# Storing the lower parts of split projection weights to device memory in the first half of the sequence and loading them in the second

## The chip, the cores and the metric

The kernel runs on one core of one Trainium2 chip. The metric is the device time of one execution in microseconds (us); smaller is better. Engines are named as in the profile: PE (TensorE matmul), PEld (its weight loads), DVE (VectorE), ACT (ScalarE), POOL (GpSimd), SP (SyncE, which issues all DMAs of this kernel).

## What is computed

A two-layer trunk on one sequence of 1024 tokens with 1024 channels, all in float32. Layer 0 is an RWKV-7 time mixer, layer 1 a diagonal state-space layer with a GLU; each is followed by a dense MLP (1024 to 4096 to 1024), and each of the four sub-layers by a layer norm. The part that matters here is the time mixer's projections:

```python
xx = jnp.pad(x, ((0, 0), (1, 0), (0, 0)))[:, :-1] - x
xr = x + xx * mu[0]; xw = x + xx * mu[1]; xk = x + xx * mu[2]
xv = x + xx * mu[3]; xa = x + xx * mu[4]; xg = x + xx * mu[5]
r = xr @ wr; k = xk @ wk; v = xv @ wv
w_pre = w0 + jnp.tanh(xw @ w1) @ w2
a = jax.nn.sigmoid(a0 + (xa @ a1) @ a2)
g = jax.nn.sigmoid(xg @ g1) @ g2
...
state = state * w_t + (state a_t) b_t + v_t k_t   # per head and token
...
h = layer_norm(ALPHA * h + (o * g) @ wo)
```

Token t of the recurrence needs r, k, v, w, a of token t and the state of token t-1. The weights are the same for all tokens.

## The kernel before, in words

**Arithmetic.** A float32 product is made of three reduced-precision (float32r) products. Every operand is split (`split`, L145): ACT copies it into a float32r tile, the upper part (`hi`), and DVE subtracts that from the original, which gives the lower part (`lo`). `mm3` (L177) then issues hi·hi, hi·lo and lo·hi into one PSUM tile.

**Weights.** `wload` (L158) brings weights in tiles of 128 x 512 (256 KB): a load to `wraw` on SP's queue (L163; 2 buffers), a cast to `whi` on ACT (L146; 3 buffers), a subtraction to `wlo` on DVE (L147; 3 buffers). The buffers of `whi` and `wlo` come free when PE has done the tile's matmuls. `WLG` (L56) is set so that no subtraction goes to POOL.

**Two halves.** The sequence is cut into two halves of 512 tokens, and `rwkv_proj(H)` (L229) makes the projections of half H with the same weights, so every weight tile is loaded and split once in each half. Through `wload` go, in each half, 2 tiles of `wa2` (`rates`, L369), 2 of `g2a` (`gate`, L384), 16 of `wk` and 16 of `wr` (`square`, L400) and 16 of `wv` (L443): 52 tiles. The results are stored to device memory by SP (`store_out`, L364; L458 for v) and loaded again by the recurrence. A few more weights (`wa1`, `g1a`, `g1c`) are scaled by mu first and go through `scaled` (L295), not through `wload`.

**Recurrence.** `core` (L757) works through 8 units: two head groups by four stretches of 256 tokens. For each: `elem` (L474; loads of r, k, sg, a at L485 and element-wise work), `amat`, `invert` (L585; a long row of small DVE operations at L608 and L610), `kbtrans`, `chain` (L645; the steps that hand the state on; loads of v at L654), `gnorm` (L701). Units 0 to 3 need the first half's projections, units 4 to 7 the second half's.

**Order.** The order on each engine's queue is made by a planner: the program is written with ranks (`rank(...)`, L86; the lower rank goes first), and the planner places instructions by a simulated timeline, by rank and by when buffers come free. Each engine, SP's DMA queue too, then works its list strictly in order. The projections of the second half (L772) and most of those of the first (L767) have rank 100000, so they fill what the units leave. After the projections come `wo`, layer norms, the MLPs and the state-space layer; these have `wload` calls of their own, which the change leaves as they are.

Of the kernel before, what the change touches and what calls it, by code (L numbers as in the profile page):

```python
# [8 lines left out]
F32 = mybir.dt.float32  # L9
# [10 lines left out]
KT = 8  # L20
# [35 lines left out]
WLG = (3, (), 0, 1)  # L56
# [14 lines left out]
def trunk(ctx, tc, A):  # L71
    nc = tc.nc
    V, S, G, PE, SP = nc.vector, nc.scalar, nc.gpsimd, nc.tensor, nc.sync

    cp = ctx.enter_context(tc.tile_pool(name="cp", bufs=1))
    dr = ctx.enter_context(tc.tile_pool(name="dr", bufs=1, space=DRAM))
# [68 lines left out]
    def split(src, hi, lo, e=None):  # L145
        S.copy(hi, src)  # L146
        (e or V).tensor_sub(lo, src, hi.bitcast(F32))  # L147
# [7 lines left out]

    nw = [0]

    def wload(src, kt, n):  # L158
        step = 512 // n
        out = []  # L160
        for k0 in range(0, kt, step):
            raw = wp.tile([128, step, n], F32, tag="wraw", name="wraw", bufs=2)
            SP.dma_start(raw, src[:, k0 : k0 + step])  # L163
            hi = wp.tile([128, step, n], F32R, tag="whi", name="whi")
            lo = wp.tile([128, step, n], F32R, tag="wlo", name="wlo")
            nw[0] += 1
            split(raw, hi, lo, G if nw[0] % WLG[0] in WLG[1] and WLG[2] <= nw[0] < WLG[3] else V)
            out += [(hi[:, k], lo[:, k]) for k in range(step)]
        return out

# [3 lines left out]
    def mmb(p, w, x, **kw):  # L174
        bulk.append((PE.matmul(p, w, x, **kw).ins, x.shape[-1]))  # L175

    def mm3(p, whi, wlo, xh, xl, first, last):  # L177
        mmb(p, whi, xh, start=first, stop=False)
        mmb(p, whi, xl, start=False, stop=False)
        mmb(p, wlo, xh, start=False, stop=last)  # L180
# [18 lines left out]
    def dense(p, w, xs):  # L199
        n = len(xs)  # L200
        for k in range(n):
            mm3(p, w[k][0], w[k][1], xs[k][0], xs[k][1], k == 0, k == n - 1)
# [11 lines left out]
    def psd():  # L214
        return pd.tile([128, HT], F32, tag="d", name="d")
# [13 lines left out]
    def rwkv_proj(H):  # L229
# [21 lines left out]
        def spare(tag, n, bufs, pool=kp):  # L251
            t = pool.tile([128, n, HT], F32R, tag=tag, name="oS", bufs=bufs)
            return [t[:, k] for k in range(n)]
# [9 lines left out]
        def mixes(j, dst=None):  # L263
            for k in range(KT):
                m = tp.tile([128, HT], F32, tag="m", name="m")
                S.mul(m, xs[k][:, 1:], mum[:, j, k : k + 1])
                if k % 4 in VM[H]:
                    V.scalar_tensor_tensor(m, xs[k][:, 0:HT], vec(f"mu{j}", k), m, op0=ALU.mult, op1=ALU.add)
                else:
                    m2 = tp.tile([128, HT], F32, tag="ev", name="m2", bufs=3)  # L270
                    G.tensor_scalar(m2, xs[k][:, 0:HT], vec(f"mu{j}", k), None, op0=ALU.mult)
                    G.tensor_add(m, m, m2)
                if dst:
                    split(m, *dst[k])
                    yield dst[k]
                else:
                    yield operand(m)
# [3 lines left out]
        if H == 0:  # L281
            hi, lo = spare("AT", KT, 1), []
# [8 lines left out]
        if H == 0:  # L291
            with rank(MIXR):
                xm = list(mixes(2))
# [30 lines left out]
        def half_sigmoid(t):  # L324
            G.tensor_scalar(t, t, 0.5, 0.5, op0=ALU.mult, op1=ALU.add)
# [38 lines left out]
        def store_out(out, n, e):  # L364
            (ST if out in STO else SP).dma_start(scr[out][n * 128 : (n + 1) * 128, t0 : t0 + HT], e)

        w2, wg = [None], [None, None]

        def rates(n):  # L369

            if n % 4 == 0:
                w2[0] = wload(A["wa2"][:, n // 4], 4, 128)
            pp = [psd(), psd()]
            for wi, xi in ((0, 0), (0, 1), (1, 0)):
                for j in range(2):
                    js = slice(64 * j, 64 * j + 64)
                    mmb(pp[j], w2[0][n % 4][wi][js], hx[xi][js], start=wi == 0 and xi == 0, stop=wi == 1)
            for j, out in ((0, "sg"), (1, "a")):
                e = tp.tile([128, HT], F32, tag="ev", name="ev", bufs=3)
                S.activation(e, pp[j], AF.Tanh, bias=pvh[:, j, n : n + 1], scale=0.5)  # L380
                half_sigmoid(e)
                store_out(out, n, e)

        def gate(n):  # L384
            if n % 4 == 0:
                wg[0] = wload(A["g2a"][:, n // 4], 4, 128)
                rawb = wp.tile([128, 512], F32, tag="wraw", name="w2raw", bufs=2)
                SP.dma_start(rawb, A["g2b"][:, n * 128 : n * 128 + 512])
                wg[1] = wp.tile([128, 512], F32R, tag="whi", name="w2st")
                S.copy(wg[1], rawb)  # L390
                V.tensor_sub(wg[1][64:128], rawb[64:128], wg[1][64:128].bitcast(F32))
            q = n % 4
            p = psd()
            mm3(p, wg[0][q][0], wg[0][q][1], gx[0], gx[1], True, False)
            mmb(p, wg[1][:, q * 128 : (q + 1) * 128], h2, start=False, stop=True)
            e = tp.tile([128, HT], F32, tag="ev", name="ev", bufs=3)
            S.copy(e, p)
            store_out("g", n, e)

        def square(wn, out, xm, n):  # L400
            p = psd()
            dense(p, wload(A[wn][n], KT, 128), xm)
            e = tp.tile([128, HT], F32, tag="ev", name="ev", bufs=3)
            S.copy(e, p)  # L404
            store_out(out, n, e)

        if H == 0:

            km = xm
            with rank(MIX0R):  # L410
                rm = list(mixes(0, spare0()))
            for n in range(4):
                rates(n)
                square("wk", "k", km, n)
            for n in range(4):
                square("wr", "r", rm, n)
            yield
            for n in range(4, KT):
                rates(n)
                square("wk", "k", km, n)  # L420
            for n in range(4, KT):
                square("wr", "r", rm, n)
            if not GV:
                for n in range(KT):
                    gate(n)
        else:
            for n in range(KT):
                rates(n)
            for n in range(KT):
                gate(n)  # L430
            xm = list(mixes(2))
            for n in range(KT):
                square("wk", "k", xm, n)
            xm = list(mixes(0))
            for n in range(KT):
                square("wr", "r", xm, n)
# [3 lines left out]
        for cb in range(4):  # L440
            pp = [psd(), psd()]
            for k0 in range(0, KT, 2):
                w = wload(A["wv"][cb][:, k0 : k0 + 2], 2, 256)  # L443
                for kk in range(2):
                    k = k0 + kk
                    for tt in range(4):
                        sl = slice(tt * 128, (tt + 1) * 128)
                        o = pp[tt // 2][:, (tt % 2) * 256 : (tt % 2) * 256 + 256]
                        mmb(o, xv[k][0][:, sl], w[kk][0], start=k == 0 and tt % 2 == 0, stop=False,
                                  skip_group_check=True)  # L450
                        mmb(o, xv[k][0][:, sl], w[kk][1], start=False, stop=False, skip_group_check=True)
                        mmb(o, xv[k][1][:, sl], w[kk][0], start=False, stop=k == KT - 1,
                                  skip_group_check=True)
            for h in range(2):
                e = tp.tile([128, 2, 256], F32, tag="ev", name="evv", bufs=3)
                S.copy(e, pp[h].rearrange("p (t n) -> p t n", t=2))
                r0 = t0 + h * 256
                SP.dma_start(scr["v"][r0 : r0 + 256, cb * 256 : (cb + 1) * 256].rearrange("(t p) n -> p t n", p=128), e)  # L458
        if H == 0 and GV:
            for n in range(KT):  # L460
                gate(n)
# [295 lines left out]
    def core():  # L757

        pg = rwkv_proj(0)
        next(pg)  # L760
        bulk.clear()
# [8 lines left out]
        for m in range(8):  # L770
            if m == PB:
                with rank(100000):  # L772
                    run(rwkv_proj(1))
# [591 lines left out]
```

## Time and profile before

| | us |
|---|---|
| median of 3 runs (lowest, highest) | 2771.85 (2769.56, 2778.86) |
| the profiled execution's own time | 2764.91 |
| its span from the first to the last instruction | 2763.2 |
| PE busy | 2604.9 (94%) |
| DVE busy | 1884.5 (68%) |
| ACT busy | 1109.5 (40%) |
| POOL busy | 719.6 (26%) |
| DMA moved | 318.63 MB, 115 GB/s on average |

The span is cut by what runs in it: set-up to 39 us, the first half's `wload` projections from 39 to 300 us, the second half's from 300 to 660 us (the units run beside both), the rest of the units with the first MLP to 1070 us, then MLPs and the state-space layer. A table by stage has, for each engine, its busy time with the number of instructions, and the granted TensorE clock as a share of full speed (PEclk). Matmuls are pipelined, so PE counts as busy also where it runs at a low clock. A line with "who <- whom" says that the first engine sat idle until the second one's instruction ended.

### The profile page before, as it was taken

Reading aid. Unit: us, or ns where it says so; the run is one execution under the profiler, and the core shown is the slowest. Engines: PE = TensorE matmul, PEld = TensorE weight load, DVE = VectorE, ACT = ScalarE, POOL = GpSimd, SP = SyncE. Lnnn points to the kernel's source line nnn. Section 1 sums busy time; section 2 is a strip of 40 time slices with the busy share of each in tenths; the row PEclk is TensorE's granted clock in tenths of the full one; section 3 lists DMA queues with packets and bytes.
Section 4 is the critical chain, followed back from the end, with each engine's and each line's share of the span. In section 5 each row is a group of like instructions: output and inputs, shape, how many; then the busy total and the mean of one; then the engine's idle time right before and its main releaser. Section 6 shows DMA issues by size and latency. Waiting matters only on the chain.

```text
span 2763.2 us, 43707 instructions
## 1 busy us (share of the span) xinstructions
PE 2604.9 (94%) x16582; PEld 2096.5 (76%) x16582; DVE 1884.5 (68%) x3242; ACT 1109.5 (40%) x1952; POOL 719.6 (26%) x601
## 2 busy tenths in 40 slices
PE   7889989889899999989999999999999999999997
PEld 5779767678677877767776788778778887788886
DVE  7487788587787777998658554574765546755556
ACT  5445454544443333334432332344323323533333
POOL 5331664450352303233122001121220101210101
PEclk9989969889889999999999999999999999999998
DMA  3543443344222323555332633223343322333333
GB/s 115 184 147 112 139 162 102 109 138 135 77 81 81 100 85 124 154 145 159 96 122 99 203 96 98 89 88 102 117 160 112 99 96 84 119 96 97 98 95 100
DMA packets 200083, 318.63 MB, mean 115 GB/s; under 512 B 19520, under 2 KB 73920, under 8 KB 199872
## 3 DMA queue, kind: packets, MB, share of 16 engines
q1 hardware_dynamic: 199872, 315.83, 36.6%
q8 instruction: 131, 2.15, 0.3%
q14 instruction: 80, 0.66, 0.1%
HBM read 265.42 MB, written 50.33 MB: 114 GB/s over the span
## 4 chain that ended last, share of the span: by engine, by line
PE 45%; DVE 5%; issue 2%; POOL 1%; DMA 1%; ACT 0%; ACTq 0%; DVEq 0%; POOLq 0%
PE d L175 40%; PE py L1219 1%; PE py L1224 1%; DVE wlo L147 1%; PE pu L152 1%; DVE t L1187 1%; PE pbu L1175 1%; DVE hA L960 0%; DVE hB L960 0%; DVE t L1185 0%; POOL rl L944 0%; PE pq L849 0%; DMA wraw<-in_mw_dram 0%; PE pu L1164 0%; DVE qbuf L147 0%
## 5 line engine op out<-in xcount | busy, mean ns | idle before, releaser
L147 DVE TENSOR_TENSOR wlo<-wraw,whi 128x512 fp32r<-128x512 f32 x720 | 535.6, 745 | 443.7 <-ACT whi L146 424.8
L146 ACT CAST whi<-wraw 128x512 fp32r<-128x512 f32 x720 | 445.7, 620 | 975.4 <-PE d L175 637.2
L175 PE MATMUL d<-qbuf,whi 128*128 128x512 f32 (+1 forms) x2112 | 655.6, 393 | 20.9 <-DVE hA L960 9.4
L175 PEld LDWEIGHTS d<-qbuf,whi 128*128 128x128 f32 x2112 | 390.3, 190 | 117.7 <-DVE hA L960 17.0
L944 POOL TENSOR_TENSOR rl<-rl 128x512 f32<-128x512 f32 x128 | 158.6, 1239 | 1058.4 <-ACT rl L943 1018.1
L175 PE MATMUL d<-qbuf,wlo 128*128 128x512 f32 (+1 forms) x1056 | 409.3, 390 | 8.2 <-DVE wlo L147 8.0
L175 PE MATMUL d<-oAh,whi 128*128 128x512 f32 (+1 forms) x960 | 387.8, 408 | 9.6 <-ACT ev L404 7.2
L175 PE MATMUL d<-oAh,wlo 128*128 128x512 f32 (+1 forms) x960 | 387.2, 406 | 5.3 <-DVE wlo L147 5.1
L175 PE MATMUL d<-oAl,whi 128*128 128x512 f32 (+1 forms) x960 | 385.5, 404 | 1.4 <-DVE oAl L147 1.4
L175 PE MATMUL d<-oBh,wlo 128*128 128x512 f32 x704 | 278.3, 396 | 1.4 <-DVE wlo L147 1.4
L175 PE MATMUL d<-oBh,whi 128*128 128x512 f32 x704 | 278.8, 396 | 0.0
L175 PE MATMUL d<-oBl,whi 128*128 128x512 f32 x704 | 276.1, 392 | 0.0
L175 PEld LDWEIGHTS d<-qbuf,wlo 128*128 128x128 f32 x1056 | 200.6, 190 | 52.8 <-DVE wlo L147 11.7
L175 PEld LDWEIGHTS d<-oAh,whi 128*128 128x128 f32 (+1 forms) x960 | 185.1, 194 | 54.2 <-ACT ev L404 9.2
L175 PEld LDWEIGHTS d<-oAh,wlo 128*128 128x128 f32 (+1 forms) x960 | 184.9, 193 | 49.1 <-DVE wlo L147 8.6
L175 PEld LDWEIGHTS d<-oAl,whi 128*128 128x128 f32 (+1 forms) x960 | 184.8, 193 | 40.6 <-DVE oAl L147 2.1
L960 DVE TENSOR_TENSOR hB<-hB,d 128x512 f32<-128x512 f32 (+1 forms) x256 | 165.2, 650 | 68.9 <-PE d L175 65.8
L960 DVE TENSOR_TENSOR hA<-hA,d 128x512 f32<-128x512 f32 x240 | 162.5, 683 | 54.5 <-PE d L175 52.5
L175 PEld LDWEIGHTS d<-oBh,wlo 128*128 128x128 f32 x704 | 132.5, 188 | 33.8 <-DVE wlo L147 2.0
L175 PEld LDWEIGHTS d<-oBl,whi 128*128 128x128 f32 x704 | 132.7, 188 | 29.4 <-issue 0.5
L175 PEld LDWEIGHTS d<-oBh,whi 128*128 128x128 f32 x704 | 132.7, 189 | 29.1 <-issue 1.5
L147 DVE TENSOR_TENSOR qbuf<-rl,qbuf 128x512 fp32r<-128x512 f32 x128 | 99.0, 774 | 70.3 <-ACT qbuf L146 69.8
(371 smaller groups left out, 3877.1 us busy)
## 6 DMA issues: line engine op xcount, KB each, us to landing
wraw<-in_mw_dram SPq DMA_DIRECT2D x520, 256.0 KB, 2.7
wraw<-in_glu_dram SPq DMA_DIRECT2D x64, 256.0 KB, 2.6
wraw<-in_wk_dram SPq DMA_DIRECT2D x32, 256.0 KB, 3.1
wraw<-in_wr_dram SPq DMA_DIRECT2D x32, 256.0 KB, 3.1
wraw<-in_wv_dram SPq DMA_DIRECT2D x32, 256.0 KB, 3.4
yl<-s_y SPq DMA_DIRECT2D x32, 256.0 KB, 3.1
wraw<-in_wo_dram SPq DMA_DIRECT2D x32, 256.0 KB, 2.8
tb<-tB SPq DMA_DIRECT2D x16, 512.0 KB, 4.9
```

The source lines that it names most:

```text
L146: S.copy(hi, src)
L147: (e or V).tensor_sub(lo, src, hi.bitcast(F32))
L152: PE.matmul(out, x, idt, start=True, stop=True)
L175: bulk.append((PE.matmul(p, w, x, **kw).ins, x.shape[-1]))
L944: G.tensor_mul(r, r, r)
L960: V.tensor_add(z, z, p)
L1175: PE.matmul(p[qs, g2, ri], tb[:, g2, ri, qs], u[:, 2 * g2 + par], start=True, stop=True)
L1187: e.tensor_mul(t2[:, :, ri], x[:, :, 1 - ri], bw[:, l, g0:g1, ri : ri + 1].broadcast_to([128, g1 - g0, n]))
L1219: PE.matmul(p[64 * j : 64 * j + 64, g2], ug[f][:, 2 * g2 + par], tv[:, par, g2], start=g2 == 0, stop=False, skip_group_check=True)
L1224: PE.matmul(p[64 * j : 64 * j + 64, g2], hb[qs, 4 * f + g2, ri, 0:NSC], tcm[qs, g2, ri], start=False, stop=ri == 1, skip_group_check=True)
```

## The change

`wload` takes a key. With a key seen for the first time (first half) the tile is split as before, and its lower part is stored as it is to a tile of its own in device memory (256 KB, on SP's queue). With a key seen before (second half) the lower part is loaded from there into `wlo` on SP's queue, and only the cast to `whi` is made. The five call sites that run once in each half pass a key; the keys are the same in both halves.

```diff
+    low = {}
+
-    def wload(src, kt, n):
+    def wload(src, kt, n, key=None):
         step = 512 // n
         out = []
         for k0 in range(0, kt, step):
+            kept = low.get((key, k0)) if key else None
             raw = wp.tile([128, step, n], F32, tag="wraw", name="wraw", bufs=2)
             SP.dma_start(raw, src[:, k0 : k0 + step])
             hi = wp.tile([128, step, n], F32R, tag="whi", name="whi")
             lo = wp.tile([128, step, n], F32R, tag="wlo", name="wlo")
             nw[0] += 1
-            split(raw, hi, lo, G if nw[0] % WLG[0] in WLG[1] and WLG[2] <= nw[0] < WLG[3] else V)
+            if kept is not None:
+                SP.dma_start(lo.bitcast(F32).rearrange("p k n -> p (k n)"), kept)
+                S.copy(hi, raw)
+            else:
+                split(raw, hi, lo, G if nw[0] % WLG[0] in WLG[1] and WLG[2] <= nw[0] < WLG[3] else V)
+                if key:
+                    low[key, k0] = dr.tile([128, 512], F32, name=f"low{len(low)}")
+                    SP.dma_start(low[key, k0], lo.bitcast(F32).rearrange("p k n -> p (k n)"))
             out += [(hi[:, k], lo[:, k]) for k in range(step)]
         return out
...
-                w2[0] = wload(A["wa2"][:, n // 4], 4, 128)
+                w2[0] = wload(A["wa2"][:, n // 4], 4, 128, f"wa2{n}")
...
-                wg[0] = wload(A["g2a"][:, n // 4], 4, 128)
+                wg[0] = wload(A["g2a"][:, n // 4], 4, 128, f"g2a{n}")
...
-            dense(p, wload(A[wn][n], KT, 128), xm)
+            dense(p, wload(A[wn][n], KT, 128, f"{wn}{n}"), xm)
...
-                w = wload(A["wv"][cb][:, k0 : k0 + 2], 2, 256)
+                w = wload(A["wv"][cb][:, k0 : k0 + 2], 2, 256, f"wv{cb}-{k0}")
```

## Rows read from the trace of the kernel before

**Rows 1.** Busy time by stage: window, PE, PEld, DVE, ACT, POOL, PEclk, DMA share, GB/s

```profile
39.00:300.00 261.00, 237.25 (x1845) 194.90 (x1844) 168.22 (x328) 128.12 (x235) 85.16 (x83) 0.94 0.45 145
300.00:660.00 360.00, 320.44 (x2933) 264.24 (x2932) 280.34 (x512) 171.15 (x320) 178.78 (x149) 0.85 0.40 127
...
1070.00:2763.00 1693.00, 1631.57 (x8504) 1307.97 (x8498) 1077.45 (x1740) 619.76 (x1051) 305.24 (x239) 0.99 0.37 114
```

**Rows 2.** SP's issues in order of time around the second half's first v

```profile
461.04 1.25 SPq L654 DMA_DIRECT2D vsa<-s_v  x2
...
619.18 0.88 SPq L458 DMA_DIRECT2D s_v<-evv  x2
...
622.68 1.33 SPq L654 DMA_DIRECT2D vsa<-s_v  x2
```

**Rows 3.** Groups of DVE's instructions by line, 300 to 660 us

```profile
L147 DVE TENSOR_TENSOR wlo<-wraw,whi 128x512 fp32r<-128x512 f32 x51 | 40.7, 801 | 30.4 <-ACT whi L146 30.2
```

**Rows 4.** What PE waited for, 300 to 660 us (total us, times, longest)

```profile
PE pU L682 <- ACT vsa L679: 5.7, 4, 2.1
...
PE d L175 <- DVE oAl L147: 4.5, 4, 2.5
PE py L747 <- DVE st L685: 4.0, 1, 4.0
PE pss L507 <- DVE AT L570: 3.0, 1, 3.0
PE d L175 <- DVE wlo L147: 2.9, 3, 1.3
```

**Rows 5.** Busy time in three shorter stretches of the second half (columns as in rows 1)

```profile
450.00:490.00 40.00, 38.13 (x294) 30.54 (x292) 35.82 (x90) 17.13 (x33) 13.15 (x10) 1.00 0.57 171
...
500.00:570.00 70.00, 67.76 (x590) 54.50 (x591) 43.51 (x68) 32.77 (x63) 34.21 (x27) 0.89 0.32 102
570.00:600.00 30.00, 19.49 (x135) 16.90 (x134) 24.77 (x40) 13.50 (x24) 18.25 (x13) 0.78 0.43 133
```

**Rows 6.** All instructions on the tile wraw, 39 to 300 us

```profile
L147 DVE TENSOR_TENSOR wlo<-wraw,whi x52: 637/691/1794, 43.5 to 271.2; 128x512 fp32r<-128x512 f32 x52
...
  DMA wraw<-in_wv_dram: 6.7, 2
  DMA wraw<-in_wr_dram: 4.5, 2
...
DMA to landing us min/median/max: 2.5/3.1/4.6
```

**Rows 7.** Issues of SP by tensor, 39 to 260 us: count, size, median us to landing

```profile
s_k<-ev SPq DMA_DIRECT2D x8, 256.0 KB, 2.6
```

**Rows 8.** SP's issues in order of time, one store

```profile
130.11 0.32 SPq L365 DMA_DIRECT2D s_sg<-ev  x1
```

**Rows 9.** What SP's queue waited for, 300 to 660 us

```profile
SPq L163 <- DVE wlo L147: 66.8, 25, 12.8
...
SPq L485 <- DVE KB L538: 19.2, 6, 5.8
```

**Rows 10.** All instructions on the tile wraw, 300 to 660 us

```profile
L163 SPq DMA_DIRECT2D wraw<-in_wv_dram x16: 327/362/954, 565.4 to 652.0; - x16
...
  DMA wraw<-in_wv_dram: 11.2, 4
  DMA wraw<-in_wr_dram: 7.1, 2
...
DMA to landing us min/median/max: 2.5/3.3/6.2
```

**Rows 11.** PE in order of time: full-clock matmuls of one weight tile

```profile
577.43 0.39 PE L175 MATMUL d<-oAh,whi 128*128 128x512 f32 x1
...
577.66 0.40 PE L175 MATMUL d<-oAl,whi 128*128 128x512 f32 x1
```

## The prediction

> **What bounds the kernel now.** First the table by stage [rows 1]. From 1070 us on PE is busy for 1631.6 of 1693 us at a clock of 0.99: nothing is to be had there, and time saved before it simply moves it forward. The first half's projections (39 to 300 us) run PE for 237.3 of 261 us at 0.94. The worst stage is the second half's projections, 300 to 660 us: PE is idle for 360 - 320.4 = 39.6 us, and its clock is 0.85, so of the 320.4 busy us about 0.15 x 320.4 = 48.1 us were lost to the low level (1.2 instead of 2.4 GHz). Some 88 us of this stage are therefore not TensorE work at full speed. DVE is busy there for 280.3 of 360 us, 78%.
>
> Does the stage's end set anything? SP's issues in order of time say so [rows 2]: the recurrence loads v at 461 us and then not before 622.7 us, 3.5 us after the first v of the second half is stored at 619.2 us. The units 4 to 7 wait for these projections, and the first MLP stands behind them on PE. Sooner projections mean sooner everything.
>
> Next, what DVE does in that stage [rows 3]: the subtractions that make `wlo` of the weights are its largest group, 51 with 40.7 us (the 52nd lies past the edge), 40.7 / 280.3 = 14.5% of its work. But PE's waits [rows 4] hardly name them: 2.9 us in 3 times. What they name is the small steps between units and bulk: a lower part of the activations (4.5), the state (4.0), the masked matrix (3.0), and pX's copies (5.7), all of them on DVE or right behind it. DVE works strictly in order, so a weight subtraction hurts through what is queued behind it. The stretches differ too [rows 5]: from 450 to 490 us DVE is busy for 35.8 of 40 us, yet PE for 38.1 at full clock, so there is little to win; from 570 to 600 us DVE has 24.8 of 30 us and PE only 19.5 at 0.78, so there is much.
>
> **The change, part by part.** Every key of the first half is asked for again in the second, so it does what it says: 52 stores, 52 loads, 52 subtractions fewer.
>
> *First half, added: 52 stores of 256 KB.* An issue of such a store occupies SP for 0.32 us [rows 8] and lands after 2.6 us [rows 7]. Each stands on SP's queue behind a wait for its subtraction; the next raw load but one waits for the same subtraction already, as that frees its `wraw`. Behind it stand other loads and the projections' own stores; if each issue delayed something on the path, it would be 52 x 0.32 = 16.6 us, the upper end. The store also holds the `wlo` buffer: 0.32 + 2.6 us after the subtraction, while PE gets to a tile only after those before it in three buffers, so PE releases later than the store and this costs nothing; without that lead it would be 2.9 us per tile. The traffic grows by 52 x 0.262 = 13.6 MB in 261 us, 52 GB/s on 145 [rows 1], 36%. ACT's waits for raw tiles there were 6.7 + 4.5 us [rows 6]; grown by 36% that is 4.0 us. About half of that is covered by buffered tiles, so I take **+2 us**, between 0 (a gain is excluded: nothing is taken off any engine in this half) and 16.6.
>
> *Second half, removed: 52 subtractions on DVE,* 0.80 us each [rows 3]. The bounds: no gain, if all of it lay beside PE's work; 52 x 0.80 = 41.6 us, if all of it were on the path. Between them I go by shares: of PE's 39.6 idle and 48.1 lost us, the part that belongs to 14.5% of DVE's work, 87.7 x 0.145 = 12.7 us. Rows 4 support the lower half of the bounds (most of DVE's work is hidden). I take **-12.7 us**. There is a page on the chip that makes the share larger: the Trainium skill (SBUF — State Buffer, "two separate sides") says that a VectorE instruction with two SBUF inputs and a GpSimd instruction that reads SBUF lock each other out for a whole instruction. The trace agrees in direction: here the subtraction takes 0.80 us on average, at its best in the first half 0.637 [rows 3, 6]. By that rule some of the freed time would be POOL's too; the sum above doesn't use it.
>
> *Second half, moved: the raw load.* It waits for a free `wraw`, which the cast on ACT now gives back, where it was the subtraction. SP stood for 66.8 us, 25 times, behind subtractions [rows 9], and ACT for 11.2 + 7.1 = 18.3 us, 6 times, behind raw tiles that came late [rows 10]. I book no gain, because the load of `wlo` now stands in the same queue and waits for PE to give back a `wlo`.
>
> *Second half, added: 52 loads of 256 KB.* On PE's side the question is whether a lower part is there in time. Matmuls follow each other at 0.23 us at full clock [rows 11]; a tile is 12 of them, 2.8 us, and with three buffers two tiles stand between the release and the next use, 5.5 us. The load needs 0.33 us to issue and 3.3 us to land, 3.6 us [rows 10], so 1.9 us are left for SP to be late, more at the low clock. With the slowest landing seen, 6.2 us, each would be 6.5 - 5.5 = 1.0 us late, 52 us at most; with the median nothing. I take **0**, by the median, and keep the upper end for a rival. What is queued behind a waiting load on SP are the units' own loads, which already stood 19.2 us behind DVE's work there [rows 9].
>
> *After 660 us:* no instruction is added or removed.
>
> Sum: +2 - 12.7 + 0 + 0 = **-10.7 us**. The profiled execution took 2764.9 us and would take 2754.2; the median of the runs is 6.9 us above it, so the prediction against the median is 2771.85 - 10.7 = **2761 us**, -0.39%. A measurement of this kernel can tell about 0.3% (8.3 us) from no change.
>
> **The rivals.**
>
> *It was hidden (no change).* PE waited for weight subtractions for only 2.9 us [rows 4], and DVE has 80 us free in the stage. If the small waits come from latency and not from DVE's queue, the gain is 2.9 us and the first half takes 2 back: 2771 us. For it: 450 to 490 us [rows 5], where DVE is full and PE does not suffer. Against it: 570 to 600 us.
>
> *The lower parts come late (slower).* The load takes the place of the wait removed: SP works in order, a load of `wlo` stands there until PE frees a buffer, and whatever stands in front delays it. It decides once a load is more than 1.9 us late after the release. Price: if half of the 52 come as late as with the slowest landing, 26 us; the first half's 4.0 in full; and -12.7 on DVE's side: +17.3 us, 2789 us. For it: raw tiles came late 6 times by 3 us each although they had a lead [rows 10]. Against it: the median landing leaves 1.9 us, and the DMA share is only 0.40 in this stage [rows 1]. Beside this stands a rule: the Trainium skill (DMA: Bandwidth & Descriptors, "Latency and other measured facts") puts an access to device memory at 0.2 us on average and 2 us at high load. By that a loaded queue would add 1.8 us, an estimate from that page, which is just the lead; the trace's landings, 2.5 at the least and 6.2 at the most [rows 10], spread wider than that.
>
> *Another plan.* The planner makes the whole order anew. One hole such as 570 to 600 us, 10.5 us of idle PE [rows 5], may vanish or open elsewhere: 10.5 us to either side of the first rival, about 2760 or 2782 us.
>
> *All on the path.* If DVE sets the pace of the whole stage, -41.6 + 2: 2732 us. Against it stand rows 4.
>
> **How the numbers follow.** The forecast 0.42, of which 0.27 lie beyond -0.3% and 0.15 within; hidden 0.20; late 0.17; another plan 0.14 (0.06 faster, 0.02 same, 0.06 slower); all on the path 0.07. Faster: 0.27 + 0.07 + 0.06 = 0.40. Same: 0.15 + 0.20 + 0.02 = 0.37. Slower: 0.17 + 0.06 = 0.23. The forecast's own range, by a share between a third of and twice 14.5%, is 2748 to 2770. The whole range goes from 2742, which leaves out the full gain and a little of the forecast, to 2787, which leaves out the worse half of the late loads: about 0.18 outside.
>
> **What the profile after would show.** Right: no subtraction of `wlo` from `wraw` between the start of the second half and the first `wo` tile; DVE's busy time there down by about 40 us; PE's idle time from 300 us to the last v store under 35 us and the clock above 0.85; the first v store of the second half some 10 us before 619 us; DMA 27 MB up. Wrong: PE waiting for a DMA into `wlo` by more than 10 us in total (late loads); first casts of the first half waiting more for raw tiles than 11 + 4 us (the stores cost more); PE's idle time unchanged with DVE freed (hidden); or the same end of the projections with other holes after 660 us (another plan).

## The result, and the profile after

The changed kernel takes 2776.23 us (median of 22 runs, 2762.75 to 2785.94), the kernel before 2768.38 beside it (22 runs, 2757.54 to 2778.86). The ratio is 1.0030, 95% interval 1.0020 to 1.0041: **slower by 8 us** (5.5 to 11.4), where 10.7 us less were forecast. The profiled execution took 2785.12 us, 9 above its median, and that of before 3.5 below its own; the two profiles therefore differ by 20 us and overstate the loss. The lines of `wload` stand up to 4 higher than before, those behind it 11.

The table by stage of the kernel after (columns as in [rows 1]); [rows 1] has the first, second and last stage of before:

```profile
39.00:300.00 261.00, 229.64 (x1663) 188.84 (x1662) 157.28 (x311) 122.34 (x221) 70.56 (x70) 0.89 0.59 185
300.00:660.00 360.00, 306.43 (x2881) 248.71 (x2879) 258.66 (x473) 165.96 (x314) 191.61 (x162) 0.86 0.51 159
...
600.00:640.00 40.00, 20.76 (x142) 19.74 (x143) 38.51 (x75) 13.15 (x23) 25.43 (x20) 0.64 0.29 95
660.00:1070.00 410.00, 390.76 (x3383) 318.03 (x3381) 314.93 (x592) 169.72 (x318) 130.18 (x104) 0.95 0.33 99
```

In the first half PE has lost 7.6 us of work and clock besides (0.89 against 0.94), while DMAs are busy for 0.59 of the time (0.45 before). In the second half DVE is relieved of 21.7 us, yet PE does 14.0 us less in the same 360 us. A third row says where: from 600 to 640 us PE is idle for almost half the time, and DVE, which the change was to relieve, is full. Before, PE had its hole at 570 to 600 us [rows 5], 10.5 us of idle time; here it is 19.2 of 40 us. A full DVE alone does not stop PE, though. Before, in the same stretch, DVE was nearly as full and PE ran on:

```profile
600.00:640.00 40.00, 38.09 (x289) 35.86 (x288) 36.87 (x80) 14.63 (x26) 13.24 (x12) 0.86 0.53 163
```

What the casts of the first half waited for (tile wraw, 39 to 300 us; [rows 6] has the same of before):

```profile
  DMA wraw<-in_wr_dram: 12.5, 6
  DMA wraw<-in_wv_dram: 10.0, 3
  DMA wraw<-in_wk_dram: 7.9, 4
...
DMA to landing us min/median/max: 2.6/3.7/6.6
```

In these lines raw tiles are late by 30.4 us in 13 times, where it was 11.2 in 4 (with the smaller lines of the view 32.8 against 11.6); they land after 3.7 us in the median, where it was 3.1.

What PE waited for from 300 to 660 us ([rows 4] of before):

```profile
PE d L186 <- DVE oAl L147: 21.2, 4, 8.3
```

The lower part of the activations, 4.5 us before, is 21.2 now. DVE in order of time in that hole (start, duration, instruction) shows what it is late behind:

```profile
608.32 1.33 DVE L619 TENSOR_TENSOR x<-xa,x 128x110 f32<-128x110 f32 x1
609.69 0.67 DVE L621 TENSOR_TENSOR x<-x 128x110 f32<-128x110 f32 x1
610.40 0.27 DVE L619 TENSOR_TENSOR x<-xa,x 128x105 f32<-128x105 f32 x1
610.71 0.27 DVE L621 TENSOR_TENSOR x<-x 128x105 f32<-128x105 f32 x1
610.89 0.69 DVE L147 TENSOR_TENSOR oAl<-m,oAh 128x512 fp32r<-128x512 f32 x1
611.49 0.28 DVE L619 TENSOR_TENSOR x<-xa,x 128x120 f32<-128x120 f32 x1
```

The inversion's small steps (L619, L621) and the activations' subtractions stand woven into each other on a queue without a gap. That weaving is the planner's choice, made anew for the changed kernel. The waits of SP's queue, 300 to 660 us ([rows 9] of before):

```profile
SPq L172 <- PE d L186: 71.2, 26, 18.4
SPq L167 <- ACT whi L173: 19.6, 11, 4.8
```

The wait for the subtraction (66.8 us before) has gone, and the load of `wlo` stands in its place and waits for PE. PE itself is not held up by late lower parts: over the whole stage the tile wlo shows 3.4 us in 2 times behind that DMA, weight loads of PE counted.

So three things are to be told apart: what the stores cost, what the missing subtractions and the loads bring, and what the new order does.

### The profile page after: what moved, and what is told of

It is laid out like the page before. It is cut to its first block, busy times and chain, and to the rows that moved or that the text cites. A ratio compares the mean times of both kernels' runs of the same rounds, so it can differ in the third digit from the quotient of the medians.

```text
span 2783.4 us, 43810 instructions
## 1 busy us (share of the span) xinstructions
PE 2605.2 (94%) x16582; PEld 2099.6 (75%) x16582; DVE 1854.5 (67%) x3190; ACT 1107.9 (40%) x1952; POOL 715.7 (26%) x601
## 4 chain that ended last, share of the span: by engine, by line
PE 45%; DVE 6%; issue 3%; DMA 1%; ACT 1%; POOL 1%; ACTq 0%; DVEq 0%; POOLq 0%; SPq 0%
PE d L186 40%; DVE wlo L147 1%; PE py L1230 1%; PE py L1235 1%; DMA wraw<-in_mw_dram 1%; POOL rl L955 1%; PE pbu L1186 1%; PE pu L152 1%; DVE hA L971 0%; ACT whi L146 0%; DVE t L1198 0%; DVE sq L856 0%; DVE t L1196 0%; PE pyt L1243 0%; PE pu L1175 0%
## 5 line engine op out<-in xcount | busy, mean ns | idle before, releaser
L146 ACT CAST whi<-wraw 128x512 fp32r<-128x512 f32 x668 | 413.7, 620 | 932.9 <-PE d L186 652.4
L147 DVE TENSOR_TENSOR wlo<-wraw,whi 128x512 fp32r<-128x512 f32 x668 | 499.6, 749 | 421.2 <-ACT whi L146 403.6
L186 PE MATMUL d<-oAh,whi 128*128 128x512 f32 (+1 forms) x960 | 389.1, 409 | 21.2 <-ACT ev L415 10.9
```

## The experiments

All are measured against the kernel before on the same chip; us are the ratio less one times the median of before there (2765.07, 2764.74, 2764.08 and 2762.01 for the four groups E1 to E4, F1 to F4, F5 to F8, G1 to G4).

| run | order | 95% interval of the ratio | us |
|---|---|---|---|
| E1 stores only | new | 1.0003 to 1.0027 | +4 |
| E2 loads, no subtraction | new | 0.9972 to 0.9998 | -4 |
| E3 neither load nor subtraction | new | 1.0018 to 1.0048 | +9 |
| E4 stores of an eighth | new | 1.0040 to 1.0066 | +15 |
| F1 whole change | old | 1.0008 to 1.0036 | +6 |
| F2 stores only | old | 1.0021 to 1.0054 | +10.5 |
| F3 loads, no subtraction | old | 0.9968 to 0.9995 | -5 |
| F4 neither load nor subtraction | old | 0.9929 to 0.9955 | -16 |
| F5 stores of an eighth | old | 1.0010 to 1.0035 | +6 |
| F6 stores behind the raw load | old | 1.0002 to 1.0038 | +5.5 |
| F7 loads on ACT's queue | old | 0.9976 to 1.0013 | -2 |
| F8 change for `wv` alone | old | 0.9993 to 1.0018 | +2 |
| G1 stores on POOL's queue | old | 1.0061 to 1.0104 | +23 |
| G2 loads behind raw loads | old | 1.0043 to 1.0081 | +17 |
| G3 work of before | that of after | 1.0065 to 1.0102 | +23 |
| G4 change, both DMAs behind raw loads | old | 1.0071 to 1.0121 | +26.5 |

### E1 to E4: parts of the change, ordered by the planner

**E1**, stores alone; the second half splits as before:

```diff
-            kept = low.get((key, k0)) if key else None
+            kept = None
...
-                if key:
+                if key and (key, k0) not in low:
```

> The first half stores all 52 lower parts (13.6 MB), the second half splits as the kernel before does and loads none of them. Traffic theory (the stores compete with the raw loads of the first half for the DMA engines): 8 to 16 us slower than before, raw tiles late for ACT by some 30 us from 39 to 300 us as in the changed kernel. Queue theory (the stores cost through SP's strict order, whatever their size): the same 8 to 16 us, so this run does not tell the two apart. Late loads (the loads of the second half cost, the stores do not): within 3 us of before. Plan theory (any edit gives another order, worth some us either way): anything within 8 us, and no relation to the 52 stores.

**E2**, loads alone: one store, and every load brings that one tile.

```diff
-                    low[key, k0] = dr.tile([128, 512], F32, name=f"low{len(low)}")
+                    new = not low
+                    low[key, k0] = dr.tile([128, 512], F32, name="low0") if new else next(iter(low.values()))
-                    SP.dma_start(low[key, k0], lo.bitcast(F32).rearrange("p k n -> p (k n)"))
+                    if new: SP.dma_start(low[key, k0], lo.bitcast(F32).rearrange("p k n -> p (k n)"))
```

> One store in all; the second half loads its 52 lower parts from that one tile (so they are not the right ones) and makes no subtraction. Traffic and queue theories: the second half alone gains, 5 to 13 us faster than before. Late loads: 5 us or more slower, PE waiting for DMA into wlo by over 10 us. Hidden theory (the subtractions never lay on the path): within 3 us.

**E3**, no store, no load, no subtraction in the second half:

```diff
-                SP.dma_start(lo.bitcast(F32).rearrange("p k n -> p (k n)"), kept)
+                lo = hi
```

> No store and no load; the second half makes no lower part of these weights at all, and PE's third product takes the upper part again (same work on PE, other numbers). It shows what 52 subtractions fewer are worth with nothing in their place. By the predicted share 13 us faster than before; hidden theory: within 3 us; if it is faster and the loading run is not, the loads eat it.

**E4**, E1 with stores of 16 of the 128 partitions:

```diff
-                    SP.dma_start(low[key, k0], lo.bitcast(F32).rearrange("p k n -> p (k n)"))
+                    SP.dma_start(low[key, k0][0:16], lo.bitcast(F32).rearrange("p k n -> p (k n)")[0:16])
```

> As the run that only stores, but of each lower part 16 of 128 partitions (32 KB): the same 52 issues, in the same place of the program, with an eighth of the traffic (1.7 MB). Traffic theory: within 3 us of before. Queue theory: 8 to 16 us slower, as with the full stores. Plan theory: no order between the two.

Measured: +4, -4, +9 and +15 us. E3 does nothing but leave work out, and is slower; E4 stores an eighth of E1's bytes, and costs more. No sum of terms gives that. Each edit makes the planner draw up another order, and by these four runs an order can be worth as much as the terms: they can't price them.

### F1 to F4: the same parts in the order of the kernel before

Each engine's list was taken from the kernel before and fixed by ordering edges that carry no semaphore; only the added DMAs are placed by the planner, between the others. The profiles bear it out: in all runs marked "old", every engine works the instructions of before in the order of before (but for one MEMSET in F4), with the added DMAs between them and the left-out subtractions missing. As in E2, the loads of F3 all bring the one stored tile, and as in E3, PE takes the upper part again in F4.

```diff
         trunk(ctx, tc, aps)
+        keep_plan(nc, tc, EXTRA, GONE)
...
+                    tc.add_manual_dep(i, prev, mybir.DependencyInfo(
+                        mybir.DependencyClass.NoSync, mybir.DependencyReason.DATA), reason="plan")
```

> The whole change, but every engine's instructions are held in the order that the planner made for the kernel before; the 52 stores and 52 loads are placed by the planner between SP's other issues, and the 52 subtractions are missing from DVE's row. Order theory (the 8 us lost by the change come from the new order that the planner made, not from the work): no slower than before, 0 to 13 us faster. Work theory (stores and loads themselves cost): 5 to 12 us slower, as the change.

> The 52 stores alone, all engines held in the order of the kernel before. It gives the price of the stores without a new order. My prediction's term: 2 us slower, bounds 0 to 16.6. Order theory: within 3 us of before. Work theory: 5 to 12 us slower.

> One store, 52 loads of that one tile into wlo in place of the 52 subtractions, all engines held in the order of the kernel before. If the loads are in time it equals the run without any lower part in the same order (by my share 13 us faster than before); if they come late it lies behind that run by the lateness, up to 20 us.

> No store, no load, no subtraction for the second half's weights (PE takes the upper part a second time), all engines held in the order of the kernel before. With the order held, less work cannot give another order. Share theory: 13 us faster. Hidden theory: 0 to 3 us faster. In an order of its own the same cut was 9 us slower than before; the difference between the two runs is the order.

Measured: +6, +10.5, -5, -16 us, and now they add up: stores and loads alone make 10.5 - 5 = +5.5, the whole change +6. Each of these is known to 4 or 5 us, so the sum agrees more closely than the runs can tell. F4 shows what the missing subtractions are worth with nothing in their place: 16 us. E3 is the same work at +9: 25 us between two orders. And F3 shows that the loads give back 16 - 5 = 11 of it, some 6 to 16 by the two intervals.

How the stores cost: tile wraw in F2, 39 to 300 us.

```profile
  DMA wraw<-in_wr_dram: 13.0, 8
  DMA wraw<-in_wk_dram: 6.4, 3
  DMA wraw<-in_wa_dram: 2.7, 1
...
  DMA wraw<-in_wv_dram: 0.4, 1
...
DMA to landing us min/median/max: 2.6/3.6/5.4
```

Raw tiles land 0.5 us later than before, and the casts wait 22.5 us for them. The mean over the stage hides how full the DMA engines are; the kernel before, then F2, from 75 to 125 us:

```profile
75.00:125.00 50.00, 48.02 (x249) 38.40 (x248) 18.85 (x28) 20.61 (x38) 13.96 (x15) 0.97 0.58 193
75.00:125.00 50.00, 45.28 (x236) 36.48 (x236) 16.49 (x25) 17.85 (x33) 10.32 (x11) 0.97 0.75 246
```

PE itself does not wait for the late casts (0.9 us in F2, 1.0 before). It waits for ACT's copy of a finished result out of PSUM, `ev`, which stands behind the casts on ACT's queue: 10.5 us in F2 from 39 to 300 us, 7.2 before. One such place in F2, ACT's instructions and then PE's; before, the same matmul had no wait:

```profile
111.92 0.62 ACT L146 CAST whi<-wraw 128x512 fp32r<-128x512 f32 x1 [3.21 <-DMA wraw<-in_wk_dram]
114.59 0.62 ACT L146 CAST whi<-wraw 128x512 fp32r<-128x512 f32 x1 [2.06 <-DMA wraw<-in_wk_dram]
115.12 0.58 ACT L415 COPY ev<-d 128x512 f32<-128x512 f32 x1
115.75 0.80 PE L186 MATMUL d<-oAh,whi 128*128 128x512 f32 x1 [1.74 <-ACT ev L415]
```

How the loads cost: F4, then F3, on tile wraw from 300 to 660 us.

```profile
  DMA wraw<-in_wk_dram: 9.9, 5
  DMA wraw<-in_wr_dram: 6.7, 3
  DMA wraw<-in_wv_dram: 6.5, 3
...
DMA to landing us min/median/max: 2.5/3.6/5.5
```

```profile
  DMA wraw<-in_wv_dram: 12.8, 5
  DMA wraw<-in_wk_dram: 10.8, 5
  DMA wraw<-in_wr_dram: 10.0, 3
...
DMA to landing us min/median/max: 2.6/4.2/6.3
```

The lower parts themselves are in time: PE waits for them for 2.6 us in 4 times in F3. It is the raw tile beside them that lands 0.6 us later, and the cast waits 33.6 us instead of 23.1. But PE does not wait for these casts either (0.3 us in F3). The units' own loads are late as well. DVE's waits for r, in F4, then in F3, and beside the latter PE's waits for lower parts (`wlo`, and `oAl` of the activations), 300 to 660 us:

```profile
DVE AR L543 <- DMA ldr<-s_r: 9.6, 4, 5.1
```

```profile
DVE AR L543 <- DMA ldr<-s_r: 14.3, 4, 6.1
PE d L186 <- DMA wlo<-low: 2.6, 4, 1.1
PE d L186 <- DVE oAl L147: 3.9, 4, 1.5
```

So the late raw tiles are seen, and how 11 us come of them is not.

PE even stands idle for less of this stage in F3 (36.5 us) than in F4 (43.7), at a lower granted clock (0.86 against 0.89). Over all their runs the mean granted clock is 0.9626 in F4 and 0.9593 both in F3 and in the kernel before; 0.0033 of 2755 us is 9 us, an estimate of what F4 has over either by its clock. By it, most of what the subtractions free, and of what the loads take back, is time at the low level and not idle time; what brings the clock down, these runs don't show.

On SP's queue the load of `wlo` stands for 75.5 us in 24 waits for PE. Whether bytes or queue make the delay, these runs leave open.

### F5 to F8: bytes, place, queue, amount

**F5** is E4 in the old order. **F6** is F2 with each store behind the raw load two tiles on, which waits for the same subtraction:

```diff
+    for store, raw in LATE:
+        tc.add_manual_dep(store, raws[raws.index(raw) + 2], mybir.DependencyInfo(
+            mybir.DependencyClass.NoSync, mybir.DependencyReason.DATA), reason="late")
```

**F7** is F3 with the loads issued by ACT, and **F8** is F1 with keys for `wv` alone, of which one of three call sites is shown (in these cuts and that of G1, what notes the added DMAs' names is left out):

```diff
-                SP.dma_start(lo.bitcast(F32).rearrange("p k n -> p (k n)"), kept)
+                S.dma_start(lo.bitcast(F32).rearrange("p k n -> p (k n)"), kept)
```

```diff
-            dense(p, wload(A[wn][n], KT, 128, f"{wn}{n}"), xm)
+            dense(p, wload(A[wn][n], KT, 128, None), xm)
```

> As the stores alone in the old order (10 us slower than before), but of each lower part only 16 of 128 partitions: all 52 issues on SP at the same places, each holding its wlo, an eighth of the traffic. Traffic theory (the stores' bytes make the raw loads land later): 0 to 3 us slower than before, raw tiles land after 3.1 us in the middle as before. Queue theory (the 52 issues ahead of the raw loads, and the hold of wlo): 7 to 10 us slower, as with whole stores.

> As the stores alone in the old order, whole, but each stands behind the raw load that waits for the same subtraction, where the planner had put it ahead. Traffic theory: 7 to 10 us slower than before all the same (the bytes are the same), at most a few us better. Queue theory: 0 to 4 us slower, since no raw load stands behind a store that became ready with it.

> As the loads alone in the old order (5 us faster than before, 11 us short of the run without any lower part), but the 52 loads are issued from ACT's queue, where the cast of the same tile waits for the same PE release anyway. If the loads cost through SP's order (a load that waits for PE holds up the raw loads and the units' loads behind it): 10 to 16 us faster than before. If they cost through the DMA engines or by being late at PE: 5 us faster, as on SP. If ACT is held up by them: slower than on SP.

> The change for wv's 16 tiles alone, in the old order. Their stores fall between 170 and 260 us, where the DMA engines are less full (share 0.4 against 0.58 at 75 to 125 us), their loads between 560 and 660 us, where PE stood idle most. Traffic theory: stores under 2 us, gain of the subtractions 16/52 of 16 us or more, loads cost a third of 11 us: 0 to 4 us faster than before. If a store costs the same everywhere: within 2 us of before.

Measured: +6, +5.5, -2, +2 us. F5 has the 52 places on SP's queue with an eighth of the bytes, and its raw tiles are as early as before:

```profile
  DMA wraw<-in_wv_dram: 4.6, 1
  DMA wraw<-in_wk_dram: 4.0, 2
  DMA wraw<-in_wr_dram: 1.1, 1
...
DMA to landing us min/median/max: 2.5/3.1/5.0
```

So F5 loses its 6 us elsewhere. In its profile the units' loads are late: from 39 to 300 us those of k and a are waited for by 16.1 and 15.8 us, 11.3 and 9.1 before. One of these waits stands on ACT ahead of an `ev` that PE needs; ACT's instruction and PE's, first before, then in F5:

```profile
81.29 0.91 ACT L503 ACTIVATE kk<-ldk,pv 128x256 f32<-128x256 f32 x2 [2.51 <-DMA ldk<-s_k]
83.24 0.50 PE L175 MATMUL d<-oAh,whi 128*128 128x512 f32 x1 [1.05 <-ACT ev L404]
```

```profile
82.30 0.91 ACT L514 ACTIVATE kk<-ldk,pv 128x256 f32<-128x256 f32 x2 [4.85 <-DMA ldk<-s_k]
84.25 0.80 PE L186 MATMUL d<-oAh,whi 128*128 128x512 f32 x1 [3.60 <-ACT ev L415]
```

F6 has the bytes without the places ahead of the raw loads, and the casts wait 9.0 us; DVE waits for its stores to give back `wlo` by 4.5 us in 2 times, which does not happen in F2. Each costs about half of F2's 10.5. That reads as two causes of 5 to 6 us that add up, the issue's place on SP's strict queue and the bytes; but the intervals of F2, F5 and F6 overlap, so neither the halves nor the adding up is shown.

F7 takes the loads and their waits off SP. Tile wraw again:

```profile
  DMA wraw<-in_wv_dram: 16.2, 5
  DMA wraw<-in_wr_dram: 9.9, 3
  DMA wraw<-in_wk_dram: 6.8, 5
...
DMA to landing us min/median/max: 2.7/4.2/6.4
```

The same landing of 4.2 us and the same waits, 32.9 us, without a place on SP: the raw tiles' lateness does not come from SP's queue, which speaks for the bytes. It is not shown for the whole 11 us: in F7 the load stands on ACT's queue instead, and no run has loads of an eighth as F5 has stores. F8, with 16 of 52 tiles, can't be told from no change.

### G1 to G4: other places, and the new order by itself

**G1** is F2 with the stores issued by POOL:

```diff
-                    SP.dma_start(low[key, k0], lo.bitcast(F32).rearrange("p k n -> p (k n)"))
+                    G.dma_start(low[key, k0], lo.bitcast(F32).rearrange("p k n -> p (k n)"))
```

**G2**: F3 with each load of a lower part behind the raw load two tiles on, by edges as in F6. **G4**: F1 with both DMAs so placed. **G3**: every engine held to the order that the planner made for the change, with the work of before; only the 52 subtractions are placed anew:

```diff
             if kept is not None:
-                SP.dma_start(lo.bitcast(F32).rearrange("p k n -> p (k n)"), kept)
                 S.copy(hi, raw)
+                d = V.tensor_sub(lo, raw, hi.bitcast(F32)).ins; EXTRA.append(d.name)
```

> The order of the kernel before is held on every engine; the first half's 52 whole stores of lower parts are added, but issued by POOL's queue instead of SP's; the second half subtracts as before. The same bytes move as in the run with the stores on SP (+10.5 us), and SP has no slot and no wait more. If the stores cost by what stands behind them on SP's queue, the cost falls from +10.5 to under +4 us, and ACT's waits for raw tiles from 39 to 300 us go from 22.5 us back to about 12. If they cost by their bytes, it stays at +7 to +11 us, with raw tiles landing after 3.5 us in the median and ACT's waits at 20 us. If POOL, whose own work now stands behind waits for DVE's subtractions, becomes late itself, it is above +11 us and PE or DVE wait for POOL in the units.

> The order of the kernel before is held; one store, 52 loads of that one tile and no subtraction in the second half, as in the run that gave -5 us; but each load of a lower part stands on SP's queue behind the raw load two tiles on, which waits for nearly the same buffer, so that no raw load stands behind a waiting load of a lower part. Without the loads the same order gave -16 us. If the 11 us are the queue, this run comes to -11 to -15 us, SP's wait of 75.5 us for PE falls under 40, and ACT's waits for raw tiles from 300 to 660 us fall from 33.6 to about 20. If they are the bytes, it stays near -5 us. If the load now comes late itself, PE waits for the DMA into wlo by more than 10 us, and the time is at or above that of the kernel before.

> The work of the kernel before, no store and no load of a lower part, in the order that the planner made for the change (every engine; only the 52 subtractions of the second half are placed anew). It prices the order by itself. By sums of the earlier runs the change costs +8 us in its own order and +6 in the old one, so the order should give +2 us, between -3 and +6. If the new order was made well for the new work and badly for the old one, it is over +6 us; if the order is what made the change slower, +8 us or more.

> The whole change in the order of the kernel before, every store and every load of a lower part on SP's queue behind the raw load two tiles on. Stores so placed gave +5.5 us, the subtractions' end -16. If the queue is what the loads cost, the sum is +5.5 - 16 + 2 = -8 us (faster than both kernels); if it is the bytes, +5.5 - 5 = 0 us; if late lower parts take its place, PE waits for the DMA into wlo by over 10 us and the time is +5 us or more.

Measured: +23, +17, +23, +26.5 us. **G1**: casts wait 21.0 us for raw tiles that land after 3.4 us, so the bytes do to them what they did on SP's queue. But the whole is worse. POOL's own work now stands behind waits (POOL's groups from 39 to 300 us: busy, mean ns, idle time ahead and for whom):

```profile
L178 POOL DMA_DIRECT2D low<-wlo x52 | 29.7, 571 | 92.9 <-DVE wlo L147 63.5 <-DVE x L619 14.1 <-DVE x L621 11.9
```

Whether that makes the difference is not shown: in this stage DVE, ACT and SP together wait for POOL by 46.0 us, where it is 38.6 in F2, and PE not at all in either.

**G2** is the rival "the lower parts come late", made to happen. PE's waits, 300 to 660 us:

```profile
PEld d L186 <- DMA wlo<-low: 28.0, 11, 5.7
...
PE d L186 <- DMA wlo<-low: 24.2, 10, 5.5
```

Issued one wait later, the loads land after 4.3 us in the median instead of 3.5, and PE stands for 24.2 us in 10 times where it was 2.6: 22 us worse than F3, by about that amount. G4 pays this and the stores. No whole change that was run beat the kernel before (F1, F8, G4); more `wlo` buffers were not tried.

**G3** prices the order. PE's waits, 300 to 660 us:

```profile
PE d L186 <- DVE oAl L147: 20.9, 4, 7.4
```

With no store and no load in the kernel, the hole of the kernel after is there, 20.9 us against 21.2, behind the same instruction; it is 3.9 us in F3. It belongs to the order. By itself it does not make a kernel slow: E2, which is 4 us faster than before, has it too (21.9 us). In that order the work of before takes 23 us more, and the work of the change takes about 23 - 8 = 15 us less than that of before; in the old order the change's work costs 6 us more. So order and work can't be added, as the +2 us expected of G3 had it: the new order suits the new work, but both together are no better than the old order with the same work (F1, +6).

## Why the prediction was wrong

**The subtractions** (-12.7 us, by their share of DVE's work): right in kind, a little small in size, and within the interval. F4 gives -16 us (-19.6 to -12.4), and as the prediction had it, part of it is idle time and part (about 9 us, by the clocks above) the low level. DVE's time on this group falls from 535.6 to 499.6 us in the whole profile. The trace of before bears out what the prediction said beside it of POOL: of these subtractions from 39 to 660 us, the 56 with no POOL instruction running beside them take 0.69 us at most, the 47 others 0.89 on average. This answers the rivals "hidden" (2.9 us) and "all on the path" (41.6): neither holds.

**The stores** (+2, bounds 0 to 16.6): the step that failed first. F2 measured +10.5 (5.8 to 14.9), inside the bounds but far from the value taken. The argument scaled 11.2 us of waits by 36% of mean traffic and halved it. The waits doubled to 22.5 us; the traffic falls in stretches that were already full (from 75 to 125 us the DMA share goes from 0.58 to 0.75), which is a likely reason. And it asked only for the casts. The places on SP's queue, for which nothing was taken, cost 6 us with an eighth of the bytes (F5), where the units' loads come late and the raw tiles do not. That the hold of `wlo` costs nothing was right: DVE does not wait for a store in F2.

**The loads** (0, "by the median landing"): the other step that failed. The lead of 1.9 us did nearly hold: PE waits for lower parts by 2.6 us in F3 and 1.5 in the kernel after. But the question was put to that tile alone. 11 of 16 us are given back, while the raw load next to it lands after 4.2 us instead of 3.6 and the units' loads of r are waited for by 14.3 us instead of 9.6. Which of these makes the 11 us stays open. By the Trainium skill (DMA: Bandwidth & Descriptors, "Latency and other measured facts") a loaded queue would add 1.8 us to an access, an estimate from its 0.2 and 2 us; the runs show 0.6 us in the median, for both kinds of placement (F3, F7), and 0.8 more on the loads in G2. The raw tiles had no lead to spare for it: in F4 the casts already waited 23.1 us for them.

**The new plan** (0 in the sum, 10.5 us to either side as a rival): the hole at 570 to 600 us shrank from 10.5 to 5.6 us, and a larger one opened at 600 to 640, as that rival said. By F1 against the kernel after it is worth +2 us on this work, within the uncertainty; E3 against F4 shows that it can be 25.

With what was measured the sum is +10.5 - 16 + 11 = +5.5, and the change in the old order gave +6. That the new order moved this by only 2 us is luck: the argument had no way to tell.

Of the signs named ahead: no subtraction of `wlo` from `wraw` is left in the second half, and DMA moves 27.3 MB more, as said. DVE's total fell by 30.0 us (1884.5 to 1854.5), not 40, as other instructions took longer. DVE's work from 300 to 660 us fell by 21.7 us; 8 of the 52 loads come after 660 us there. PE's idle time from 300 us to the last v store (712.9 us) is 54.3 us instead of under 35, its clock there 0.87, and the first v of the second half is stored late, not early:

```profile
646.87 0.36 SPq L469 DMA_DIRECT2D s_v<-evv  x1
...
712.93 0.38 SPq L469 DMA_DIRECT2D s_v<-evv  x1
```

That is 27.7 us behind [rows 2]. The sign "first casts waiting for raw tiles by more than 11 + 4 us" came true, at 30.4 us: the stores cost more.

## What to carry to other kernels

A transfer that takes the place of a computation can be paid by its neighbours, as here: look at the lead of all the loads that run beside it, in the busiest stretch and not in the mean of a stage. Where a planner makes the order, hold the order fixed before pricing a part; here an edit that only left work out cost 9 us in its own order and gained 16 in the old one. Work taken off a queue that is full of small dependent steps gained 16 us here, and the stores and loads that it needed cost 21.

## What was not expected of the hardware

256 KB loads on SP's queue land later, with 52 more of the same size in 360 us, by 0.6 us in the median, although the mean DMA share is only 0.54 (F3; 0.42 in F4), and the median is the same whether SP or ACT issues the added ones. A store of 256 KB from POOL's queue occupies POOL for 0.571 us and lands after 3.9 us (G1), where SP's took 2.4 (F2).
